# A hybrid decoder block: the state's update put ahead of the decay matrices' products, and the MLA heads' operands cast and split in two pieces

## The chip, the cores and the metric

One core of a Trainium2 chip. The metric is the device time of one execution in microseconds (us); the median of several executions is compared. TensorE (PE), VectorE (DVE), ScalarE (ACT) and GpSimd (POOL) each work through a queue of their own, in order; SP and ACT issue the DMAs.

## What is computed

One layer of a decoder trunk on 1,040 tokens (16 learned ones and 1,024 real ones), width 1,024. Three mixers stand side by side: stick-breaking attention (8 heads), a Mamba-2 state space mixer (SSD, 16 heads of 64, state 128, two groups), and MLA attention (8 heads, 64 + 32 columns per query and key). The two parts that the change touches:

```
# SSD, in chunks of 128 tokens; per group g of 8 heads
y_diag = einsum('bclsgj,bcsgjp->bclgjp', CB[..., None] * Ldec, X)
states = einsum('bclgn,bclgjp->bcgjpn', Bc, X * decay[..., None])
carry  = carry * chunk_decay + states              # chunk after chunk
y_off  = einsum('bclgn,bcgjpn->bclgjp', Cc, prev) * exp(Acs)
y      = y_diag + y_off

# MLA
s = einsum('bqhd,bkhd->bhqk', q, k) * scale        # q, k: 96 columns
o = softmax(mask(s)) @ v
```

After the mixers come the output projection and a gated feed-forward layer, each with a residual sum, and a last norm.

## The kernel before

Each dense product is made of three matmuls on fp32r operands, split in a high and a low half: `dense_fm` (L139 to L152; the matmuls are L147 to L149). Two PSUM banks (`d_ps`, pool `dpool`) take turns there; the engine that evacuates one sets when it is free.

A scheduler of the framework sets the order in which each engine gets its instructions. It goes through a simulated time line, and takes what is ready by the order in the program and by the priorities in it; so dense matmuls of later steps stand among the matmuls of the SSD chunks and of the MLA heads wherever these were not ready in its time line. They are called the fill here. What fills the SSD chunks is the latents' projection, the values `vtok` (L915 to L917) and the heads' key and query projections; what fills the MLA heads is the gate's projection (`gate_units`) and then the output projection (`out_rows`).

**SSD** (`ssd_chunk`, L765 to L856). Nine chunks, c = 0 to 8 (c = 0 has 16 tokens, and no `yo`, `yd` and `y`), each with two groups g. A group's chain:

- PE: eight small matmuls into two banks `R` (L802), which spread the running sums of the decays.
- ACT: `ea` (L811, four instructions: exp of the sums), `L` (L814, eight; then one exp over all of it, L824), and in between `dec` (L819).
- DVE: `L` times the masked product of the chunk's B and C (`cbm`, L829).
- PE: `yo` (L834, four matmuls): the chunk's C times the state `S[g]` as it stood before the chunk. DVE multiplies `ea` by it (L835).
- PE: `yd` (L838, eight matmuls): the decay matrices' products, X times `L`.
- POOL: `y += ea` (L843), then DVE: `y += yd` (L844).
- PE: `sps` (L847): the chunk's share of the state, from `Xd` (POOL, L820). POOL multiplies `S[g]` by the chunk's decay (L851), DVE adds `sps` (L854).

`yo`, `yd` and `sps` take turns in the two banks of the pool `yps`. There is one buffer for `ea` (tag `yt`, `bufs=1`): ACT writes a group's `ea` only when POOL has read the one of the group before. On POOL there stand, beside these, `y = xs * dsk` of a later chunk (L773), the low halves of weights (L136) and sums of squares (`grow`, L521).

**MLA** (`mla_load`, L963 to L980). Per head, the query (96 x 1024) and the key (96 x 1040) come by DMA into `st`, ACT casts each into `mhi` (L977), and POOL subtracts into `mlo` (L978). `mla_row` makes the scores from them (L997 to L999) and the exponentials `pr` on ACT (L1012); `weighted_values` transposes these (L319 to L331) and multiplies them by the values.

Of the kernel before, what the change touches and what calls it, by code (L numbers as in the profile page):

```python
# [11 lines left out]
F32 = mybir.dt.float32  # L12
# [3 lines left out]
ALU = mybir.AluOpType  # L16
# [43 lines left out]
def tile_hybrid_block(ctx: ExitStack, tc: tile.TileContext, a: dict):  # L60
    nc = tc.nc
    act, dve, pool, pe, sp = nc.scalar, nc.vector, nc.gpsimd, nc.tensor, nc.sync
# [6 lines left out]
    def f32(ap):  # L69
        return ap.bitcast(F32)  # L70
# [679 lines left out]
    with ExitStack() as st:  # L750
# [4 lines left out]
        yps = st.enter_context(tc.tile_pool(name="yps", bufs=2, space=PSUM, reuse_waits="tile"))  # L755
# [8 lines left out]
        def ssd_chunk(c):  # L764
            n = META if c == 0 else 128  # L765
            t0 = 0 if c == 0 else META + 128 * (c - 1)
            xs = p2.tile([128, 8, 128], F32, tag="xs", name="xs")
            bc = p2.tile([128, 4, 128], F32, tag="bc", name="bc")
            sp.dma_start(bc[:, :, :n], s_xs[8:12, :, t0 : t0 + n].rearrange("j p t -> p j t"))
            sp.dma_start(xs[:, :, :n], s_xs[0:8, :, t0 : t0 + n].rearrange("j p t -> p j t"))  # L770
            if c > 0:
                y = p2.tile([128, 8, 128], F32, tag="y", name="y")
                pool.tensor_tensor(y, xs, dsk.unsqueeze(2).to_broadcast([128, 8, 128]), op=ALU.mult)  # L773
            X = p2.tile([128, D], F32, tag="X", name="X")
            Xd = p2.tile([128, D], F32, tag="Xd", bufs=1, name="Xd")
            for g in range(2):
                gs = slice(512 * g, 512 * (g + 1))
                hs = slice(8 * g, 8 * g + 8)
                pt = tp.tile([128, 512], F32, tag="tp", name="xtp")
                for e in range(4):  # L780
                    pe.transpose(pt[:n, e * 128 : (e + 1) * 128], xs[:, 4 * g + e, :n], ident)
                dve.tensor_tensor(
                    heads(X[:n, gs]), heads(pt[:n]), DT[:n, c, hs].unsqueeze(2).to_broadcast([n, 8, 64]), op=ALU.mult
                )
            if c < 8:
                btok = p2.tile([128, 256], F32, tag="btok", bufs=1, name="btok")
                pt = tp.tile([128, 512], F32, tag="tp", name="btp")
                for g in range(2):
                    pe.transpose(pt[:n, g * 128 : (g + 1) * 128], bc[:, g, :n], ident)
                act.copy(btok[:n], pt[:n, :256])  # L790
            for g in range(2):
                gs = slice(512 * g, 512 * (g + 1))
                hs = slice(8 * g, 8 * g + 8)
                cd = p2.tile([128, 8], F32, tag="cd", name="cd")
                dec = p2.tile([128, 8], F32, tag="dec", name="dec")
                L = p2.tile([128, 8, 128], F32, tag="L", name="L")
                ea = p2.tile([128, 4, 128], F32, tag="yt", bufs=1, name="ea")
                for q in range(2):
                    R = rps.tile([128, 4, 128], F32, tag="R", name="R")
                    qs = slice(4 * q, 4 * q + 4)  # L800
                    for h in range(4):
                        pe.matmul(R[:, h, :n], sel[:, 8 * g + 4 * q + h, :], A3[:, t0 : t0 + n], start=True, stop=True)  # L802
                    if c < 8:
                        act.activation(cd[:, qs], R[:, :, n - 1], AF.Exp)
                        dve.tensor_tensor(
                            dec[:n, qs], R[:n, :, n - 1], AT[:n, c, 8 * g + 4 * q : 8 * g + 4 * q + 4], op=ALU.subtract
                        )
                    if c > 0:
                        for e in range(2):
                            half = slice(64 * e, 64 * e + 64)  # L810
                            act.activation(ea[half, 2 * q : 2 * q + 2], R[half, e::2, :], AF.Exp)  # L811
                        for h in range(4):
                            hh = 4 * q + h
                            act.activation(  # L814
                                L[:, hh, :], R[:, h, :], AF.Relu, scale=-1.0,
                                bias=AT[:, c, 8 * g + hh : 8 * g + hh + 1],
                            )
                if c < 8:
                    act.activation(dec[:n], dec[:n], AF.Exp)  # L819
                    pool.tensor_tensor(  # L820
                        heads(Xd[:n, gs]), heads(X[:n, gs]), dec[:n].unsqueeze(2).to_broadcast([n, 8, 64]), op=ALU.mult
                    )
                if c > 0:
                    act.activation(L, L, AF.Exp, scale=-1.0)  # L824
                    pcb = tp.tile([128, 512], F32, tag="tp", name="cbp")
                    pe.matmul(pcb[:, :128], bc[:, g, :], bc[:, 2 + g, :], start=True, stop=True)
                    cbm = p2.tile([128, 128], F32, tag="cbm", name="cbm")
                    dve.tensor_tensor(cbm, pcb[:, :128], tri, op=ALU.mult)
                    dve.tensor_tensor(L, L, cbm.unsqueeze(1).to_broadcast([128, 8, 128]), op=ALU.mult)  # L829
                    yo = yps.tile([128, 512], F32, tag="y", name="yo")  # L830
                    yd = yps.tile([128, 512], F32, tag="y", name="yd")
                    for j in range(4):
                        ts = slice(128 * j, 128 * (j + 1))
                        pe.matmul(yo[:, ts], S[g][:, ts], bc[:, 2 + g, :], start=True, stop=True)  # L834
                    dve.tensor_tensor(ea, ea, yo.rearrange("p (j t) -> p j t", j=4), op=ALU.mult)  # L835
                    for h in range(8):
                        hh = 8 * g + h
                        pe.matmul(  # L838
                            yd[64 * (h % 2) : 64 * (h % 2) + 64, 128 * (h // 2) : 128 * (h // 2 + 1)],
                            X[:, hh * 64 : (hh + 1) * 64], L[:, h, :], start=True, stop=True,  # L840
                        )
                    yg = y[:, 4 * g : 4 * g + 4]
                    pool.tensor_tensor(yg, yg, ea, op=ALU.add)  # L843
                    dve.tensor_tensor(yg, yg, yd.rearrange("p (j t) -> p j t", j=4), op=ALU.add)  # L844
                if c < 8:
                    sps = yps.tile([128, 512], F32, tag="y", name="sps")
                    pe.matmul(sps, btok[:n, g * 128 : (g + 1) * 128], Xd[:n, gs], start=True, stop=True)  # L847
                    if c == 0:
                        dve.tensor_copy(S[g], sps)
                    else:  # L850
                        pool.tensor_tensor(  # L851
                            heads(S[g]), heads(S[g]), cd.unsqueeze(2).to_broadcast([128, 8, 64]), op=ALU.mult
                        )
                        dve.tensor_tensor(S[g], S[g], sps, op=ALU.add)  # L854
            if c > 0:
                act.dma_start(s_y[:, :, 128 * (c - 1) : 128 * c].rearrange("j p t -> p j t"), y)  # L856

# [52 lines left out]
        for b, (t0, w) in enumerate(BLOCKS):  # L910
# [7 lines left out]
            t = row_tile("vtok")  # L918
# [18 lines left out]
        for c0, n in CH_SHORT:  # L937
            c = slice(c0, c0 + n)
# [3 lines left out]
            for half, (op, ta, tb) in enumerate(((ALU.subtract, ct, sn), (ALU.add, sn, ct))):  # L942
                t = fill_tile("cacc", "rope")
# [15 lines left out]
    with ExitStack() as st:  # L959
# [5 lines left out]
        def mla_load(h):  # L965
            p, hr = h // 2, slice(64 * (h % 2), 64 * (h % 2) + 64)
            out = []
            for cols, parts in (
                (SEQ, [(s_qn[p, hr], 0, 64), (s_qr[0, 16 * h : 16 * h + 16], 64, 80), (s_qr[1, 16 * h : 16 * h + 16], 80, 96)]),
                (T, [(s_kn[p, hr], 0, 64), (s_krot, 64, 96)]),  # L970
            ):
                raw = ml.tile([128, T], F32, tag="st", name="st")
                for src, r0, r1 in parts:
                    sp.dma_start(raw[r0:r1, :cols], src)
                hi = ml.tile([128, T], F32R, tag=f"hi{cols}", name="mhi")
                lo = ml.tile([128, T], F32R, tag=f"lo{cols}", name="mlo")
                act.copy(hi[:96, :cols], raw[:96, :cols])  # L977
                pool.tensor_tensor(lo[:96, :cols], raw[:96, :cols], f32(hi[:96, :cols]), op=ALU.subtract)  # L978
                out += [hi, lo]
            return out  # L980

# [143 lines left out]
    cols = ctx.enter_context(tc.tile_pool(name="cols", bufs=1, side="right", reuse_waits="tile"))  # L1125
# [69 lines left out]
    for kt in range(4):  # L1195
        hi, lo = homes[kt]
# [581 lines left out]
```

## Time and profile before

| | |
|---|---|
| three executions | 1761.19, 1754.87, 1760.85 us; median 1760.85 |
| the profiled execution | 1762.44 us, of which its span is 1760.7 us |
| busy in the span | PE 1706.4 us (97%), DVE 1140.2, ACT 846.2, POOL 720.0 |
| granted TensorE clock, mean | 0.986 of 2.4 GHz |
| SSD chunks, from the first `yo` to the last | 490.4 to 637.4 us |
| MLA heads, scores | 665.7 to 1001.1 us |

In the time line of the profile a row is an instruction or several that were merged: its start and duration in us, the engine, the line, the operation, and in brackets how long the engine was idle just before and what ended that. A matmul's duration overlaps with the next one's; how far PE gets is read from the starts.

### The profile page before, as it was taken

The page shows a single profiled execution, that of the slowest core. Times are in us where ns is not written, and L with a number is a line of the kernel's source. Part 1 is how long each engine was busy: PE and PEld are TensorE (multiplying, and loading weights), DVE is VectorE, ACT ScalarE, POOL GpSimd, SP SyncE. Part 2 cuts the span into 40 slices and gives each one's busy share as a digit, 9 for nine tenths or more (in the row PEclk, how much of TensorE's full clock was granted, in tenths as well). Part 3 has the DMA queues.
Part 4 walks back from the last instruction along what each step waited for, and adds up shares of the span by engine and source line. Part 5 has one row for each costly group of instructions (what it writes and reads, how often), then busy time and mean ns, then how long its engine had stood idle before and what let it go on. Part 6 is the DMA issues. An engine that isn't in the chain of part 4 may idle for free. (4 is left out here: it accounts for less than half of the span.)

```text
span 1760.7 us, 26573 instructions
## 1 busy us (share of the span) xinstructions
PE 1706.4 (97%) x9801; PEld 1500.3 (85%) x9801; DVE 1140.2 (65%) x1742; ACT 846.2 (48%) x1797; POOL 720.0 (41%) x498
## 2 busy tenths in 40 slices
PE   8979999999999899999999999999999999999998
PEld 7969989999987788998888888778888888878887
DVE  7778666678444663555575655986566666688644
ACT  7546565655467646675454425432222232244332
POOL 3334346344466657563321346544455545200012
PEclk9989999999999999999999998999999999999998
DMA  4312232122533645347330443123333223999702
GB/s 162 82 56 64 71 86 79 58 71 73 156 111 115 200 157 154 108 125 244 110 91 29 124 155 102 60 84 101 109 102 102 96 90 104 314 370 386 254 1 97
DMA packets 145639, 222.35 MB, mean 126 GB/s; under 512 B 24722, under 2 KB 84148, under 8 KB 145508
## 3 DMA queue, kind: packets, MB, share of 16 engines
q1 hardware_dynamic: 126112, 205.09, 35.9%
q10 hardware_dynamic: 19396, 15.56, 2.9%
q8 instruction: 77, 1.26, 0.3%
q14 instruction: 54, 0.44, 0.1%
HBM read 157.56 MB, written 63.04 MB: 125 GB/s over the span
## 5 line engine op out<-in xcount | busy, mean ns | idle before, releaser
L147 PE MATMUL d_ps<-hnh,whi 128*128 128x384 f32 (+6 forms) x744 | 250.1, 336 | 7.4 <-DVE KS L610 4.7
L149 PE MATMUL d_ps<-hnl,whi 128*128 128x384 f32 (+6 forms) x744 | 246.7, 332 | 0.0
L148 PE MATMUL d_ps<-hnh,wlo 128*128 128x384 f32 (+6 forms) x744 | 245.8, 330 | 0.0
L136 POOL TENSOR_TENSOR wlo<-wraw,whi 128x1024 fp32r<-128x1024 f32 (+1 forms) x57 | 138.0, 2420 | 222.7 <-ACT whi L134 218.3
L147 PEld LDWEIGHTS d_ps<-hnh,whi 128*128 128x128 f32 (+1 forms) x744 | 141.0, 190 | 12.5 <-issue 6.1
L148 PEld LDWEIGHTS d_ps<-hnh,wlo 128*128 128x128 f32 (+1 forms) x744 | 141.2, 190 | 2.8 <-issue 0.5
L149 PEld LDWEIGHTS d_ps<-hnl,whi 128*128 128x128 f32 (+1 forms) x744 | 140.9, 189 | 2.8 <-issue 0.2
L1285 PE MATMUL b_ps<-T,wl 128*128 128x512 f32 x352 | 138.8, 394 | 1.3 <-POOL wl L1116 1.3
L1286 PE MATMUL b_ps<-T,wh 128*128 128x512 f32 x352 | 138.2, 394 | 1.3 <-DVE T L1116 1.3
L1284 PE MATMUL b_ps<-T,wh 128*128 128x512 f32 x352 | 139.1, 396 | 0.0
L315 DVE TENSOR_TENSOR pl<-ptg,ph 128x512 fp32r<-128x512 f32 (+1 forms) x160 | 99.3, 627 | 48.2 <-ACT ph L314 46.9
L1115 ACT CAST op<-raw 128x1024 fp32r<-128x1024 f32 x69 | 71.3, 1050 | 107.4 <-PE d_ps L1570 59.2
L1116 DVE TENSOR_TENSOR op<-raw,op 128x1024 fp32r<-128x1024 f32 x69 | 84.8, 1239 | 39.0 <-ACT op L1115 38.9
L704 DVE TENSOR_TENSOR_SCAN cm<-cm,zcol 128x144 f32<-128x144 f32 (+3 forms) x64 | 101.7, 1593 | 12.3 <-ACT cm L702 11.9
L314 ACT CAST ph<-ptg 128x512 fp32r<-128x512 f32 (+1 forms) x160 | 85.2, 543 | 39.9 <-PE ptg L331 24.7
L1116 POOL TENSOR_TENSOR wlo<-raw,whi 128x1024 fp32r<-128x1024 f32 x18 | 45.6, 2531 | 110.0 <-ACT whi L1115 110.0
L1116 POOL TENSOR_TENSOR wl<-raw,wh 128x512 fp32r<-128x512 f32 x46 | 74.4, 1625 | 29.2 <-ACT wh L1115 29.2
L1115 ACT CAST wh<-raw 128x512 fp32r<-128x512 f32 x88 | 53.1, 615 | 67.2 <-PE b_ps L1286 67.1
L1122 POOL TENSOR_TENSOR tt<-tt 128x512 f32<-128x512 f32 (+1 forms) x8 | 8.1, 1011 | 186.1 <-ACT tt L1640 185.9
L1012 ACT ACTIVATE pr<-sc_ps,sm 128x256 f32<-128x256 f32 (+4 forms) x112 | 59.8, 540 | 46.8 <-DVE sm L1009 24.8
L1285 PEld LDWEIGHTS b_ps<-T,wl 128*128 128x128 f32 x352 | 66.5, 189 | 16.8 <-POOL wl L1116 1.6
L502 DVE SCALAR_TENSOR_TENSOR cacc<-d_ps,cw,cacc 128x384 f32<-128x384 f32 (+3 forms) x108 | 61.7, 571 | 29.5 <-ACT cacc L495 27.4
(442 smaller groups left out, 5180.8 us busy)
## 6 DMA issues: line engine op xcount, KB each, us to landing
raw<-in_w_down_dram SPq DMA_DIRECT2D x99, 256.0 KB, 5.3
s_hops<-gs SPq DMA_DIRECT2D x63, 256.0 KB, 2.0
raw<-s_hops SPq DMA_DIRECT2D x63, 256.0 KB, 5.4
raw<-in_w_gate_dram SPq DMA_DIRECT2D x22, 512.0 KB, 3.6
raw<-in_w_up_dram SPq DMA_DIRECT2D x22, 512.0 KB, 4.1
wraw<-in_w_o_dram SPq DMA_DIRECT2D x16, 512.0 KB, 4.5
wraw<-in_w_xbc_dram SPq DMA_DIRECT2D x12, 512.0 KB, 3.6
s_xs<-csig SPq DMA_DIRECT2D x24, 192.0 KB, 1.9
```

Of the source, the lines that this page charges most:

```text
L136: pool.tensor_tensor(lo[:, :cols], raw[:, :cols], f32(hi[:, :cols]), op=ALU.subtract)
L147: pe.matmul(ps[:m, :n], wh, mh, start=(kt == 0), stop=False)
L148: pe.matmul(ps[:m, :n], wl, mh, start=False, stop=False)
L149: pe.matmul(ps[:m, :n], wh, ml, start=False, stop=(kt == nkt - 1))
L314: act.copy(ph[:, :n], pt[:, :n])
L315: dve.tensor_tensor(pl[:, :n], pt[:, :n], f32(ph[:, :n]), op=ALU.subtract)
L704: dve.tensor_tensor_scan(rev, rev, zcol.to_broadcast([128, n_all]), 1.0, ALU.mult, ALU.add)
L1115: act.copy(hi, value)
L1116: eng.tensor_tensor(lo, value, f32(hi), op=ALU.subtract)
L1284: pe.matmul(banks[j], hi[:, ks], UH[u][k], start=start and k == 0, stop=False, skip_group_check=skip)
L1285: pe.matmul(banks[j], lo[:, ks], UH[u][k], start=False, stop=False, skip_group_check=skip)
L1286: pe.matmul(banks[j], hi[:, ks], UL[u][k], start=False, stop=stop and k == 3, skip_group_check=skip)
```

## The change

In `ssd_chunk` the block from `sps` to the sum into `S[g]` stands ahead of the block with `yd` and the two sums into `y`. In `mla_load` each operand is cast and split in two pieces of columns, 0 to 511 and the rest (512 or 528).

```diff
                     yo = yps.tile([128, 512], F32, tag="y", name="yo")
-                    yd = yps.tile([128, 512], F32, tag="y", name="yd")
                     for j in range(4):
                         ts = slice(128 * j, 128 * (j + 1))
                         pe.matmul(yo[:, ts], S[g][:, ts], bc[:, 2 + g, :], start=True, stop=True)
                     dve.tensor_tensor(ea, ea, yo.rearrange("p (j t) -> p j t", j=4), op=ALU.mult)
-                    for h in range(8):
-                        hh = 8 * g + h
-                        pe.matmul(
-                            yd[64 * (h % 2) : 64 * (h % 2) + 64, 128 * (h // 2) : 128 * (h // 2 + 1)],
-                            X[:, hh * 64 : (hh + 1) * 64], L[:, h, :], start=True, stop=True,
-                        )
-                    yg = y[:, 4 * g : 4 * g + 4]
-                    pool.tensor_tensor(yg, yg, ea, op=ALU.add)
-                    dve.tensor_tensor(yg, yg, yd.rearrange("p (j t) -> p j t", j=4), op=ALU.add)
                 if c < 8:
                     sps = yps.tile([128, 512], F32, tag="y", name="sps")
                     pe.matmul(sps, btok[:n, g * 128 : (g + 1) * 128], Xd[:n, gs], start=True, stop=True)
...
                         dve.tensor_tensor(S[g], S[g], sps, op=ALU.add)
+                if c > 0:
+                    yd = yps.tile([128, 512], F32, tag="y", name="yd")
+                    for h in range(8):
+                        hh = 8 * g + h
+                        pe.matmul(
+                            yd[64 * (h % 2) : 64 * (h % 2) + 64, 128 * (h // 2) : 128 * (h // 2 + 1)],
+                            X[:, hh * 64 : (hh + 1) * 64], L[:, h, :], start=True, stop=True,
+                        )
+                    yg = y[:, 4 * g : 4 * g + 4]
+                    pool.tensor_tensor(yg, yg, ea, op=ALU.add)
+                    dve.tensor_tensor(yg, yg, yd.rearrange("p (j t) -> p j t", j=4), op=ALU.add)
...
-                act.copy(hi[:96, :cols], raw[:96, :cols])
-                pool.tensor_tensor(lo[:96, :cols], raw[:96, :cols], f32(hi[:96, :cols]), op=ALU.subtract)
+                for c in (slice(0, 512), slice(512, cols)):
+                    act.copy(hi[:96, c], raw[:96, c])
+                    pool.tensor_tensor(lo[:96, c], raw[:96, c], f32(hi[:96, c]), op=ALU.subtract)
                 out += [hi, lo]
```

The scheduler then moves more than the block. In the new program's lines `sps` is L837, `S` L841, `yd` L849, `y += ea` L854, `y += yd` L855, the casts L979 and L980, the scores L999 to L1001.

The first place is PE in the SSD chunks, at chunk 6's first group. Before (`yd` of the group, and `sps` right behind it):

```order
L149 MATMUL d_ps_7408<-llo_7234,whi_7351 128x272
L838 MATMUL yd_6358<-L_6321,X_6300 64x128 x8
L847 MATMUL sps_6374<-Xd_6301,btok_6314 128x512
L147 MATMUL d_ps_7416<-lhi_7227,whi_7351 128x384
L148 MATMUL d_ps_7416<-lhi_7227,wlo_7353 128x384
L149 MATMUL d_ps_7416<-llo_7228,whi_7351 128x384
```

The same place in the changed program:

```order
L149 MATMUL d_ps_7356<-llo_7234,whi_7351 128x272
L789 MATMUL btp_6459<-identr_88,bc_6439 128x128 x2
L849 MATMUL yd_6367<-L_6321,X_6300 64x128 x8
L833 MATMUL yo_6416<-bc_6295,S1_5504 128x128 x4
L826 MATMUL cbp_6496<-bc_6439 128x128
L147 MATMUL d_ps_7364<-lhi_7227,whi_7351 128x384
```

The next group's `yo` stands right behind `yd` now, and `sps` of this group stands some 20 rows ahead of this `yd`. The fill is an earlier one: from the first `yo` to the last there are 144 fill matmuls of 384 columns, 66 of 256 and 24 of 272 in either program, but 54 of 512 columns where there were 117; the other 63 stand behind the chunks.

The second place is POOL at chunk 4 (`y_6010`; `ea_6034` and `ea_6093` are its two groups, and `y_6154` is chunk 5's). Before:

```order
L820 TENSOR_TENSOR Xd_6013<-X_6012,dec_6032 128x512
L170 TENSOR_TENSOR rc_7209<-rc_7209,mhalf_96 128x8
L851 TENSOR_TENSOR S0_5503<-S0_5503,cd_6031 128x512
L773 TENSOR_TENSOR y_6154<-xs_6150,dsk_5501 128x1024
L843 TENSOR_TENSOR y_6010<-y_6010,ea_6034 128x512
L820 TENSOR_TENSOR Xd_6013<-X_6012,dec_6091 128x512
L851 TENSOR_TENSOR S1_5504<-S1_5504,cd_6090 128x512
L843 TENSOR_TENSOR y_6010<-y_6010,ea_6093 128x512
```

Now:

```order
L841 TENSOR_TENSOR S0_5503<-S0_5503,cd_6031 128x512
L820 TENSOR_TENSOR Xd_6013<-X_6012,dec_6032 128x512
L854 TENSOR_TENSOR y_6010<-y_6010,ea_6034 128x512
L136 TENSOR_TENSOR wlo_7353<-wraw_7349,whi_7351 128x1024
L521 TENSOR_TENSOR grow_5484<-grow_5484,sq_7197 128x256
L773 TENSOR_TENSOR y_6154<-xs_6150,dsk_5501 128x1024
L841 TENSOR_TENSOR S1_5504<-S1_5504,cd_6090 128x512
L854 TENSOR_TENSOR y_6010<-y_6010,ea_6093 128x512
```

The scaling of `xs` moves behind the first group's `y += ea`, and stands, with a weight's low half and a sum of squares, ahead of the second group's. It moves behind `y += ea` of the first group in the same way at chunk 6 (`y_6442`, chunk 7's, behind `ea_6322`), and stays ahead of it at chunk 3 (`y_6010`, with a sum of squares, ahead of `ea_5890`) and at chunk 7 (`y_6586` ahead of `ea_6466`).

The third place is ACT where the sixth MLA head's operands are cast, at the end of the gate's fill. Before:

```order
L314 CAST ph_8878<-ptg_8874 128x384
L977 CAST mhi_9338<-st_9335 96x1040
L977 CAST mhi_9331<-st_9327 96x1024
L339 COPY half_8886<-pv_8841 64x256
L1012 ACTIVATE pr_8908,sm_8909<-sc_ps_8910,sm_8909 128x272
```

Now:

```order
L1014 ACTIVATE pr_8907,sm_8908<-sc_ps_8914,sm_8908 128x512
L979 CAST mhi_9360<-st_9357 96x512
L979 CAST mhi_9360<-st_9357 96x528
L979 CAST mhi_9351<-st_9347 96x512 x2
L339 COPY half_8902<-pv_8857 64x256
L1014 ACTIVATE pr_8924,sm_8925<-sc_ps_8926,sm_8925 128x272
```

The four pieces stand in a row, with nothing of another kind between them; so they do at all eight heads on ACT, but for one pair of the second head, and in POOL's queue the pieces of one operand stand together as well.

## Rows read from the trace of the kernel before

**Rows 1.** The page's first part: busy time, share of the span and number of instructions of PE and its weight loads.

```profile
PE 1706.4 (97%) x9801; PEld 1500.3 (85%) x9801; DVE 1140.2 (65%) x1742; ACT 846.2 (48%) x1797; POOL 720.0 (41%) x498
```

**Rows 2.** Busy time of each engine in stretches: start and end, length, PE, its weight loads, DVE, ACT, POOL (with instructions), granted clock, DMA share, GB/s. Two stretches of 10 us, then the SSD chunks from the first `yo` to the last.

```profile
540.00:550.00 10.00, 7.47 (x50) 6.46 (x51) 4.23 (x6) 7.86 (x24) 7.35 (x6) 0.68 0.26 81
820.00:830.00 10.00, 9.42 (x53) 9.26 (x54) 4.55 (x8) 5.84 (x17) 4.81 (x3) 0.66 1.03 331
...
490.40:637.40 147.00, 137.37 (x1010) 114.32 (x1009) 84.76 (x138) 96.49 (x277) 92.75 (x64) 0.98 0.45 143
```

**Rows 3.** What PE waited for between 470 and 660 us: us in total, times, longest.

```profile
PE yd L838 <- DVE L L829: 4.7, 8, 1.2
PE R L802 <- ACT L L814: 2.3, 4, 1.4
PE yo L834 <- DVE y L844: 1.4, 1, 1.4
PE d_ps L176 <- ACT lrow L743: 0.6, 1, 0.6
PE d_ps L149 <- DVE llo L881: 0.4, 1, 0.4
```

**Rows 4.** What ACT and POOL waited for between 500 and 645 us, the longest of each.

```profile
ACT ea L811 <- POOL y L843: 22.3, 9, 4.0
...
POOL y L843 <- DVE ea L835: 10.2, 4, 5.7
```

**Rows 5.** The time line at chunk 3: POOL, then ACT and PE.

```profile
534.45 2.37 POOL L773 TENSOR_TENSOR y<-xs,dsk 128x1024 f32<-128x1024 f32 x1 [3.37 <-issue]
536.78 1.04 POOL L851 TENSOR_TENSOR S<-S,cd 128x512 f32<-128x512 f32 x1
537.78 1.00 POOL L521 TENSOR_TENSOR grow<-grow,sq 128x384 f32<-128x384 f32 x1
538.75 1.27 POOL L843 TENSOR_TENSOR y<-y,ea 128x512 f32<-128x512 f32 x1
...
540.06 0.77 ACT L811 ACTIVATE ea<-R 64x256 f32<-64x256 f32 x2 [4.01 <-POOL y L843]
...
543.84 0.58 PE L802 MATMUL R<-A,sel 80*128 80x128 bf16 x4 [1.42 <-ACT L L814]
```

**Rows 6.** The time line at chunk 6: POOL, ACT, and the three waits of PE.

```profile
594.13 1.90 POOL L773 TENSOR_TENSOR y<-xs,dsk 128x1024 f32<-128x1024 f32 x1 [6.12 <-DVE nope L894]
595.99 1.04 POOL L851 TENSOR_TENSOR S<-S,cd 128x512 f32<-128x512 f32 x1
596.99 1.27 POOL L843 TENSOR_TENSOR y<-y,ea 128x512 f32<-128x512 f32 x1
...
598.30 0.77 ACT L811 ACTIVATE ea<-R 64x256 f32<-64x256 f32 x2 [3.72 <-POOL y L843]
...
599.04 1.16 PE L834 MATMUL yo<-bc,S 128*128 128x128 f32 x8 [1.37 <-DVE y L844]
602.08 0.38 PE L802 MATMUL R<-A,sel 80*128 80x128 bf16 x4 [0.39 <-ACT L L814]
604.43 1.09 PE L838 MATMUL yd<-L,X 128*64 128x128 f32 x16 [0.86 <-DVE L L829]
```

**Rows 7.** PE's time line: `yo` of chunk 5's two groups, and two fill matmuls of 512 columns.

```profile
571.46 1.11 PE L834 MATMUL yo<-bc,S 128*128 128x128 f32 x8
579.39 0.78 PE L834 MATMUL yo<-bc,S 128*128 128x128 f32 x5
...
555.19 0.39 PE L917 MATMUL d_ps<-wlo,lhi 128*16 128x512 f32 x1
555.42 0.39 PE L915 MATMUL d_ps<-whi,lhi 128*16 128x512 f32 x1
```

**Rows 8.** Groups of instructions by line and form: busy us, mean ns of one, idle before. The MLA operands' casts and splits, and pieces of 512 columns of the same kind elsewhere.

```profile
L977 ACT CAST mhi<-st 96x1024 fp32r<-96x1024 f32 x8 | 8.4, 1044 | 4.2 <-DMA st<-s_qr 3.8 <-DMA st<-s_kn 0.4
L1115 ACT CAST wh<-raw 128x512 fp32r<-128x512 f32 x88 | 53.1, 615 | 67.2 <-PE b_ps L1286 67.1
L978 POOL TENSOR_TENSOR mlo<-st,mhi 96x1024 fp32r<-96x1024 f32 x8 | 19.1, 2392 | 0.8 <-ACT mhi L977 0.8
L231 POOL TENSOR_TENSOR wk<-raw,wk 128x512 fp32r<-128x512 f32 x1 | 1.3, 1277 | 4.0 <-ACT wk L230 4.0
L1116 POOL TENSOR_TENSOR wl<-raw,wh 128x512 fp32r<-128x512 f32 x46 | 74.4, 1625 | 29.2 <-ACT wh L1115 29.2
```

**Rows 9.** The time line at the first MLA head (POOL, DVE) and at the sixth head's casts (ACT, PE).

```profile
664.17 4.82 POOL L978 TENSOR_TENSOR mlo<-st,mhi 96x1024 fp32r<-96x1024 f32 x2
668.93 1.04 POOL L548 TENSOR_TENSOR gy<-gy,gs 128x384 f32<-128x384 f32 x1
...
670.00 0.56 DVE L550 TENSOR_TENSOR go<-d_ps,gy 128x384 f32<-128x384 f32 x1 [5.20 <-POOL gy L548]
...
817.52 2.00 ACT L977 CAST mhi<-st 96x1040 fp32r<-96x1040 f32 x2 [0.64 <-PE sc_ps L998]
...
820.58 0.38 PE L319 MATMUL ptm<-identr,pr 128*16 128x128 f32 x1 [2.00 <-ACT pr L1012]
```

**Rows 10.** What PE waited for between 660 and 1040 us, the longest.

```profile
PE ptm L319 <- ACT pr L1012: 2.2, 2, 2.0
```

## The prediction

> **What bounds the kernel now.** The page's first part comes first: PE is busy 1706.4 us, 97% of the span, and the next engine, DVE, 65% [rows 1]. So the time changes only where PE waits or where its clock falls. The matmuls are the same before and after; an earlier operand anywhere else is worth nothing unless a wait of PE ends with it. The change touches two stages, and each is read by itself.
>
> The SSD chunks last 147.0 us from the first `yo` to the last [rows 2]: 16 groups, 15 periods of 9.8 us. ACT is busy there 96.5 us, POOL 92.75, DVE 84.8, some 6 us of each group, so none of the three is full. PE's waits of that stage are five kinds, 4.7 + 2.3 + 1.4 + 0.6 + 0.4 = 9.4 us [rows 3]; and in one stretch of 10 us the granted clock is 0.68, between the two levels of 1.2 and 2.4 GHz, which costs at most 10 x 0.32 = 3.2 us [rows 2]. What stands behind most of these waits is seen on ACT: it waits 22.3 us in 9 times to write `ea`, because POOL has not yet read the one before; and POOL waits 10.2 us for DVE's product [rows 4]. There is one buffer for `ea`. Where POOL has something else ahead of `y += ea`, this loop stretches. At chunk 3 that is the scaling of `xs` (2.37 us), `S` and a sum of squares: ACT waits 4.01 us, and PE 1.42 us soon after [rows 5]. At chunk 6 the scaling begins at 594.13 and `y += ea` only at 596.99; ACT waits 3.72 us, and PE 1.37 + 0.39 + 0.86 = 2.6 us at three places until 604.43 [rows 6].
>
> In the MLA heads the reader is to look for a wait of PE on the split operands. There is none among the longest; the longest is of the transposes for `pr`, 2.2 us in two times [rows 10].
>
> **Part 1, the state's block ahead of the decay matrices' products.** The block is one matmul (`sps`), one POOL multiplication (`S`) and one DVE sum per group, with no DMA; `yd`, `y += ea` and `y += yd` slip behind it, and behind the last of these the store of `y`, whose reader comes long after the chunks. No instruction is added, so the direct cost is nothing; what counts is order.
>
> *On POOL.* At chunk 6 the scaling of `xs` moves behind the first group's `y += ea`. That sum can then start some 1.9 us earlier, at about the end of `S`, which itself needed only PE's `yo` [rows 6]. The 1.37 us of `yo` go twice over: it waited for the bank which `y += yd` freed, and now the banks turn as `yo`, `sps`, `yd`, so that the next `yo` takes over the bank of `sps`. ACT's `ea` and `L` follow earlier, and the 0.39 and 0.86 us behind them go too: **-2.6 us**. At chunk 3 the scaling and the sum of squares still stand ahead of `y += ea`, and I leave the waits of 1.42 us and the low clock as they are [rows 5]. At chunk 4 the scaling goes behind the first `y += ea` but comes to stand, with a weight's low half, ahead of the second: a gain and a loss of the same size, taken as 0.
>
> *On PE.* Between the first `yo` and the last there are 63 fill matmuls of 512 columns fewer. One of these takes 0.23 us by the starts of two neighbours, 555.19 and 555.42 [rows 7]. So 63 x 0.23 = 14.5 us of fill move behind the chunks. They cost PE the same there; the stage would be shorter by 14.5 us if nothing else set its pace. PE's own work in the stage is 147.0 - 9.4 = 137.6 us now, and 137.6 - 14.5 = 123.1 us then, 8.2 us per group. Can the other engines keep that? The quickest group in the trace took 579.39 - 571.46 = 7.9 us [rows 7], and the three engines' busy shares of 6 us allow it. The ends: if every wait goes, -9.4 us (with the clock, -12.6); if the groups keep their 9.8 us although the fill is gone, +14.5 us. The point at which nothing is won or lost is a mean period of (123.1 + 9.4) / 15 = 8.8 us. I take the groups to follow at about that pace, since the fastest period lies below it and the mean of 9.8 contains 0.97 us of fill that leaves it and 0.6 us of waits: 9.8 - 0.97 is the same 8.8. So nothing for this and the 2.6 us from chunk 6 remain.
>
> A rule bears on this stage. The Trainium skill, Perfetto Trace Analysis, section Optimization Strategy, takes consistent bubbles as a sign of too few buffers; the change adds none, so by that rule the stage would keep its waits (rival B). The row with one buffer's wait, 22.3 us on ACT, speaks for it.
>
> **Part 2, the casts and splits in two pieces.** Eight heads with two operands each get 16 casts and 16 subtractions more. On ACT a piece of 512 columns takes 615 ns where it is of the same kind elsewhere, the whole 1044 ns: 2 x 615 - 1044 = 186 ns more per operand, 0.37 us per head. On POOL a subtraction of 512 columns took 1277 or 1625 ns, the whole 2392 ns: 0.16 to 0.86 us more per operand, 0.3 to 1.7 us per head [rows 8]. What can it gain? A score could start on the first piece; but no wait of PE for a split operand is among the trace's [rows 10], so 0. What can it cost? It costs where ACT's or POOL's burst delays somebody. One such place is at 817.52: two casts of 2.00 us in a row, and PE waits 2.00 us for `pr` at 820.58 [rows 9]; the clock of that stretch is 0.66 [rows 2]. With four pieces in a row, as they stand on ACT, the burst is 0.37 us longer, and so is the wait. The other is at the first head: POOL's two subtractions take 4.82 us, then comes `gy` at 668.93, and DVE's `go`, which frees the fill's bank, waits 5.20 us for that [rows 9]. There I take the lower price, 2 x 0.16 = 0.32 us, since 1277 ns is nearest to half of 2392. Elsewhere ACT (48%) and POOL (41%) have room [rows 1]. Together **+0.7 us**; bounds are -2.0 (the wait at 820.58 goes) and 0.37 + 1.7 = +2.1.
>
> A rule speaks for the split. The Trainium skill, Perfetto Trace Analysis, section Optimizing Scalar/DVE Operations, advises to break up instructions where Scalar or Vector are not saturated but cause bubbles on other engines. By it the wait behind the burst would halve, -1.0 in place of +0.37; that would need something to pass between the pieces, and the order has them back to back.
>
> **Sum.** The profiled execution took 1762.4 us. 1762.4 - 2.6 + 0.7 = 1760.5. It stands 1.6 us above the median of the runs shown, 1760.85; so against that median I forecast 1760.5 - 1.6 = **1758.9 us**, 0.1% less. A measurement of this kernel can tell about 0.5% from no change, 8.8 us.
>
> **The rivals.**
> *A, the forecast*: the chunk 6 waits go, the rest keeps pace. Its own range is 1753 to 1765 (1758.9 and 6 to either side, half of the stage's ends). Chance 0.42.
> *B, nothing happens*: the one buffer for `ea` goes on setting the waits, in other places than before, as POOL's order moves a stall from one group to the next; the stage keeps its 9.4 us. 1762.4 + 0.7 - 1.6 = 1761.5. For it: the buffer is untouched, and the scaling merely changes its place at chunk 4. Against it: chunk 6. Chance 0.15.
> *C, all waits go*: with the banks' turn changed and `S` earlier, no group waits any more, and the clock does not fall either: 1762.4 - 9.4 - 3.2 + 0.7 - 1.6 = 1748.9. For it: the largest kind, `yd` behind `L` (4.7 us), gets more room, as `sps` now stands some 20 rows ahead of `yd`. Against it: chunk 3's order stays. Chance 0.26.
> *D, slower*: the order puts the groups closer together, with less fill between them, than the loop over `ea` (ACT, DVE, POOL, ACT) lets them go. PE then waits out the time in which fill stood before. If the groups keep 9.8 us, all 14.5 us turn into waits: 1762.4 + 14.5 + 0.7 - 1.6 = 1776.0. It decides from a period of 8.8 us on, and is worth 0.5% from (123.1 + 9.4 + 8.1) / 15 = 9.4 us. For it: ACT's 22.3 us of waiting show that the loop, not ACT's work, sets its pace already. Against it: the period of 7.9 us. Chance 0.17.
>
> **How the numbers follow.** A and B lie within 0.5%: 0.57. C is faster by over 0.5%: 0.26. D is slower by that: 0.17. The range goes from a little below C (1748.9, less 3.9 for a clock that holds elsewhere too, since 820 to 830 shows 0.66 as well) to the middle of the way from A to D and somewhat beyond, at a period of 9.5 us: 1745 to 1772. Left out is the upper half of D and what no case holds.
>
> **What would show it.** Right: in the chunks the first `yo` to the last take about 130 us; ACT's waits for `ea` fall from 22 us, and at chunk 6 PE has no wait of over 0.5 us at `yo`; at chunk 3 the 1.42 us and the low clock are there still; PE has the 63 fill matmuls behind the chunks at 0.23 us each; the cast's pieces take some 0.6 us, and PE's longest wait for `pr` is 2.0 to 2.4 us. Wrong: a stage of 140 us or more with waits for `L`, `ea` or a bank of over 15 us (D); a stage below 124 us (C); PE waiting for a piece `mlo` or `mhi`, which part 2 says never occurs; or a difference in the gate, the output projection or the feed-forward layer, where I count nothing.

## The result

The changed kernel took 1749.45 us (median of 8 executions, 1742.89 to 1751.59), the kernel before 1760.07 us (8 executions). The ratio is 0.9937, with a 95% interval of 0.9925 to 0.9949: 0.6% faster, outside the 0.5% that the forecast of 1758.9 us stood for. The time lies in the range, on the side of rival C. It did not get there in rival C's way alone.

### The profile page after: what moved, and what is told of

It reads as the page before. It is cut to its first block, busy times and chain, and to the rows that moved or that the text cites. A ratio compares the mean times of both kernels' runs of the same rounds, so it can differ in the third digit from the quotient of the medians.

```text
span 1745.5 us, 26611 instructions
## 1 busy us (share of the span) xinstructions
PE 1697.1 (97%) x9801; PEld 1491.2 (85%) x9801; DVE 1136.4 (65%) x1742; ACT 847.0 (49%) x1813; POOL 717.3 (41%) x514
## 5 line engine op out<-in xcount | busy, mean ns | idle before, releaser
L134 ACT CAST whi<-wraw 128x1024 fp32r<-128x1024 f32 (+1 forms) x57 | 58.9, 1034 | 58.7 <-PE d_ps L149 33.5
L1121 DVE TENSOR_TENSOR raw<-raw 128x512 f32<-128x512 f32 x58 | 54.3, 947 | 42.2 <-DMA raw<-in_w_gate_dram 39.5
L1288 PEld LDWEIGHTS b_ps<-T,wh 128*128 128x128 f32 x352 | 66.3, 188 | 16.6 <-DVE T L1118 1.6
```

The source lines that it names most:

```text
L1288: pe.matmul(banks[j], hi[:, ks], UL[u][k], start=False, stop=stop and k == 3, skip_group_check=skip)
```

## The profile after

The profiled execution took 1747.19 us. Its page's first part, against [rows 1]:

```profile
PE 1697.1 (97%) x9801; PEld 1491.2 (85%) x9801; DVE 1136.4 (65%) x1742; ACT 847.0 (49%) x1813; POOL 717.3 (41%) x514
```

The 9801 matmuls are the same, yet PE is busy 9.3 us less. The span fell by 15.2 us, so PE's idle time fell only by 5.9. The same matmuls in less time points to the clock: the mean granted clock is 0.986 before and 0.993 after. Part of the 15.2 is the two executions: the first `yo` comes 3.1 us earlier although everything up to there is the same.

The table by stages needs two cuts that mean the same in both programs: the first `yo`, the first score, and the first matmul of the feed-forward layer's second product. Between these PE has the same 3739 matmul records in both. Columns as in [rows 2]; before:

```profile
490.38:665.66 175.28, 164.29 (x1173) 139.65 (x1173) 97.75 (x163) 109.60 (x304) 105.29 (x76) 0.98 0.47 148
665.66:1108.90 443.24, 434.57 (x2567) 388.88 (x2567) 252.78 (x493) 236.30 (x544) 188.68 (x121) 0.98 0.40 121
```

After, with the chunks alone (first `yo` to the last) in the third row:

```profile
487.27:659.07 171.80, 163.26 (x1170) 138.61 (x1169) 94.31 (x163) 107.89 (x303) 105.25 (x76) 0.98 0.47 150
659.07:1094.70 435.63, 428.93 (x2570) 383.55 (x2571) 252.45 (x494) 238.47 (x560) 187.88 (x137) 0.99 0.40 124
...
487.27:610.45 123.18, 119.40 (x947) 100.16 (x947) 71.16 (x130) 94.20 (x277) 84.41 (x61) 1.00 0.45 139
```

So 3.5 us went in the first stretch and 7.6 us in the second, which the prediction had down for +0.7. PE's idle time is the length less its busy time. It fell from 10.99 to 8.54 us in the first stretch and from 8.67 to 6.70 in the second; the other 1.0 and 5.6 us are PE being busy for less time with all but the same matmuls, an estimate of what the clock gave.

**The chunks.** They last 123.2 us instead of 147.0, a period of 8.2 us, which is the pace that the prediction worked out for PE without any wait. That the two agree is partly luck: PE still idles 123.18 - 119.40 = 3.8 us of it, and the low clock that the prediction's 137.6 us contained (3.2 us) is not there. What PE waited for, from the first `yo` to the feed-forward layer (us, times, longest), against [rows 3] (the kinds of the heads are left out):

```profile
PE d_ps L147 <- ACT lrow L743: 2.7, 1, 2.7
...
PE d_ps L176 <- DVE nope L895: 1.4, 1, 1.4
PE d_ps L147 <- DVE rope L946: 1.2, 1, 1.2
...
PE yd L849 <- DVE L L829: 0.9, 2, 0.6
PE sc_ps L999 <- ACT mhi L979: 0.8, 1, 0.8
...
PE R L802 <- ACT L L814: 0.4, 1, 0.4
```

`yd` behind `L` fell from 4.7 us in 8 times to 0.9 in 2. One group (chunk 5's second) shows how. Before: DVE finishes `L` at 584.62, and PE, which had been standing there for 1.13 us, starts `yd` at 584.67.

```profile
582.61 2.01 DVE L829 TENSOR_TENSOR L<-L,cbm 128x1024 f32<-128x1024 f32 x1 [1.31 <-ACT L L824]
...
584.67 1.09 PE L838 MATMUL yd<-L,X 128*64 128x128 f32 x16 [1.13 <-DVE L L829]
```

The same group after: `L` is done at 569.39, and PE comes to `yd` 1.67 us later, without a wait, since matmuls of other work now stand ahead of it.

```profile
567.74 1.65 DVE L829 TENSOR_TENSOR L<-L,cbm 128x1024 f32<-128x1024 f32 x1 [2.71 <-ACT L L824]
...
571.06 1.09 PE L849 MATMUL yd<-L,X 128*64 128x128 f32 x16
```

At chunk 3 the loop over `ea` is as it was in [rows 5]: the scaling and the sum of squares stand ahead of `y += ea`, and ACT waits 3.65 us. But no wait of PE of over 0.4 us is left behind it:

```profile
526.71 1.90 POOL L773 TENSOR_TENSOR y<-xs,dsk 128x1024 f32<-128x1024 f32 x1 [0.57 <-DMA s_y<-y]
528.57 1.00 POOL L521 TENSOR_TENSOR grow<-grow,sq 128x384 f32<-128x384 f32 x1
529.52 1.27 POOL L854 TENSOR_TENSOR y<-y,ea 128x512 f32<-128x512 f32 x1
...
530.83 0.77 ACT L811 ACTIVATE ea<-R 64x256 f32<-64x256 f32 x2 [3.65 <-POOL y L854]
```

From the last `yo` to the first score it then takes 48.6 us instead of 28.3: 14.5 us of it are the 63 fill matmuls, and the rest is mostly one new wait, 2.67 us for a row of norms (`lrow`), with a low clock behind it (PE's row, then stretches with the granted clock as in [rows 2]):

```profile
614.28 0.79 PE L147 MATMUL d_ps<-lhi,whi 128*128 128x512 f32 x1 [2.67 <-ACT lrow L743]
```

```profile
614.00:615.00 1.00, 0.72 (x2) 0.63 (x3) 1.00 (x1) 1.00 (x3) 0.79 (x2) 0.50 0.74 290
615.00:620.00 5.00, 5.00 (x14) 3.84 (x13) 3.94 (x2) 0.66 (x1) 5.00 (x2) 0.50 0.26 104
```

So of 23.8 us won in the chunks 14.5 are fill that stands elsewhere, and some 6 are given back there (2.67 of the wait, and by an estimate 3 of a clock at half of 2.4 GHz).

At the very end of that stretch stands one of the prediction's own signs of being wrong: the first score waits for a piece `mhi`, which part 2 says never occurs.

```profile
659.07 0.68 PE L999 MATMUL sc_ps<-mhi 96*128 96x144 f32 x3 [0.85 <-ACT mhi L979]
```

**The heads.** The sixth head, where [rows 9] had a burst of two casts and PE's wait of 2.00 us for `pr`:

```profile
809.89 2.19 ACT L979 CAST mhi<-st 96x512 fp32r<-96x512 f32 x4 [0.91 <-PE sc_ps L1000]
...
811.46 2.05 PE L176 MATMUL d_ps<-identr,rc 128*128 128x128 f32 x16 [1.06 <-POOL rc L170]
813.34 0.27 PE L319 MATMUL ptm<-identr,pr 128*16 128x128 f32 x1
```

ACT's burst is longer (2.19 us for four pieces), as the prediction said. But PE does not wait for `pr` there: 16 matmuls of the gate's norms, which before stood behind this place (from 822.57 on), fill it, after a wait of 1.06 us of their own. The clock of 0.66 in the stretch behind it is gone (1.00 from 812 to 822).

## The experiments

Ratios are against the kernel before, timed beside them, with 95% intervals.

**The two parts alone.** The first kernel keeps the whole operands, the second the old chunks.

```diff
 # e1: as the changed kernel, but in mla_load
-                for c in (slice(0, 512), slice(512, cols)):
-                    act.copy(hi[:96, c], raw[:96, c])
-                    ...
+                act.copy(hi[:96, :cols], raw[:96, :cols])
+                pool.tensor_tensor(lo[:96, :cols], raw[:96, :cols], f32(hi[:96, :cols]), op=ALU.subtract)
```

> Only the state's block is moved; the MLA operands stay whole. Theory 1 (the two parts act separately, each in its own stage): from the first yo to the first score the trace of the changed kernel was 3.5 us shorter, so about 1756.5 us against 1760.1 before; the wait of 2.0 us for pr at the sixth head and the low clock behind it are still there. Rival (the moved block alone brings everything, because the 63 fill matmuls that moved behind the chunks fill the MLA heads' gaps): about 1749.5 us, and no wait of 2 us at the sixth head.

Measured: 1756.81 us, 0.9981 (0.9969 to 0.9992).

> Only the casts and splits are in two pieces; the chunks' order is that of before. Theory 1: from the first score to the feed-forward layer the changed kernel was 7.6 us shorter, so about 1752.5 us, the chunks keep about 175 us from the first yo to the first score, and there is no wait of over 0.5 us for pr at the sixth head. Rival (the moved block brings everything): 1760.1 to 1761 us, as the prediction's second part had it (+0.7 us).

Measured: 1752.47 us, 0.9956 (0.9938 to 0.9973). The product of the two ratios is 0.9937, the ratio of both together: the parts add up, and theory 1 holds in size. The orders show why they can: e1's order on PE is that of the changed kernel through the chunks but for four rows, e2's is that of the changed kernel from the first score to the end. But e1's order in the heads is neither before's nor the changed kernel's, so the moved block does not act on the chunks alone. The same stretches, e1 first, then e2:

```profile
490.70:661.06 170.36, 161.43 (x1173) 137.26 (x1173) 94.45 (x163) 108.17 (x303) 105.69 (x76) 1.00 0.48 152
661.06:1103.80 442.74, 431.00 (x2566) 385.38 (x2566) 255.71 (x493) 236.00 (x545) 188.67 (x121) 0.98 0.40 122
```

```profile
488.02:662.23 174.21, 163.37 (x1170) 138.33 (x1169) 98.56 (x163) 108.73 (x304) 104.72 (x76) 0.98 0.46 148
662.23:1101.80 439.57, 432.03 (x2570) 386.02 (x2571) 253.10 (x494) 238.26 (x560) 188.04 (x137) 0.98 0.40 123
```

The rows show less than the times do. Of the 7.2 us between e2's profile and before's only 3.7 lie in the heads' stretch, and only 1.1 of these are idle time (8.67 and 7.54); 2.4 us lie ahead of the first `yo`, where PE's order is the same.

e1 wins 4.9 us in the first stretch, where its clock is 1.00 all along although PE waits 2.6 us for `lrow` there as well, and in the second PE's idle time is 442.74 - 431.00 = 11.7 us, 3.1 more than before. Most of that is one place, at the end of the output projection, where nothing else is left for PE:

```profile
1030.38 0.80 PE L1386 MATMUL d_ps<-raw,whi 128*128 128x512 f32 x1 [3.04 <-DVE hT L1095]
```

Before has no such wait, nor have e2 and the changed kernel, where 12 matmuls of `out_rows` are left to stand between the last product's first matmuls and this one.

**A second buffer for `ea`**, in the changed kernel (`bufs=1` to `bufs=2` on tag `yt`).

> The changed kernel with two buffers for ea instead of one. Theory 1 (what is left of waits in the chunks comes from other places: lrow, the rotary and norm rows): the waits of ACT for ea (11.7 us) go, PE gets back at most the 0.9 + 0.5 + 0.4 us for L and ea; 1747.5 to 1749.5 us. Rival (the one buffer sets the stage's pace, the row of ACT's waits for ea): all 6.5 us of waits in the chunks and the 3.3 us of low clock at 613 to 620 go, about 1740 us.

Measured: 1748.19 us, 0.9935 (0.9917 to 0.9953), the changed kernel's ratio. ACT's 11.7 us of waits for POOL's `y += ea` go, and 13.7 us of waits for DVE's `dec` stand in their place. The order changed with the buffer: the chunks last only 112.65 us, more fill stands behind them, and PE waits 4.0 us for `lhi` there. Up to the first score it is 170.55 us with 8.99 us of idle time, where the changed kernel has 171.80 and 8.54. So the buffer's waits were not what kept PE idle in the changed kernel, and the rival falls. That they were not in the kernel before is argued from this and from chunk 3: no run gave that kernel a second buffer. Its trace has other links as long beside those of [rows 4], where POOL's longest wait is not shown:

```profile
ACT dec L819 <- DVE dec L805: 13.8, 8, 3.3
...
POOL Xd L820 <- ACT dec L819: 10.8, 3, 5.5
```

**What of the split counts?** Six kernels vary the pieces in the changed kernel, with the chunks as they are.

```diff
 # e4: casts in pieces, one subtraction
+                for c in (slice(0, 512), slice(512, cols)):
+                    act.copy(hi[:96, c], raw[:96, c])
+                pool.tensor_tensor(lo[:96, :cols], raw[:96, :cols], f32(hi[:96, :cols]), op=ALU.subtract)
 # e5: one cast, subtractions in pieces
 # e6, e8: in pieces for h != 5, for h == 0
 # e7: pieces of 256 columns
 # e9: whole for h in (3, 5, 6, 7)
```

> The changed kernel with the casts in two pieces, but one whole subtraction on POOL per operand. Theory 1a (the order that follows from ACT's pieces is the gain, not the pieces' earlier ends): 1749 to 1750 us, as the changed kernel. Rival 1b (POOL's pieces let the scores start earlier): the gain of the MLA heads goes, about 1756.5 us, and PE waits for mlo or pr over 1 us somewhere in the heads.

Measured: 1751.07 us, 0.9951 (0.9934 to 0.9969). By the time the subtraction's pieces can be left out: the interval overlaps the changed kernel's and ends below rival 1b's 1756.5 us, though 1a's own range is missed by 1 us. Its cause does not follow: the order in the heads is another one than the changed kernel's, and PE waits 1.8 us for `mhi` and 3.4 us for `pr` in the heads (0.8 and 1.7 in the changed kernel).

> The changed kernel with whole casts on ACT and only POOL's subtractions in two pieces. But for 34 rows at the first heads PE's order is that of the kernel with the moved block alone (1756.8 us). Theory S1 (the gain of the heads comes from the order that the scheduler makes when ACT's casts are in pieces: it fills places where PE waited, and the low clock behind them goes): about 1757 us, with the wait of 2.0 us for pr at the sixth head. Rival S2 (the pieces' earlier ends are the gain): some of the 7.7 us, 1750 to 1754 us.

Measured: 1753.6 us, 0.9968 (0.9956 to 0.9981). The time lies in S2's range of 1750 to 1754 us; the interval overlaps e1's as well: undecided by the time. In its profile the heads' stretch is 443.1 us (e1 442.7), with the 2.0 us for `pr` and a wait of 3.4 us at the output projection's end; its span gained on e1's ahead of the first `yo`, where the programs are alike.

> The changed kernel with the sixth head's operands whole again, the other seven in pieces. PE's order is that of the changed kernel but for four rows. S1 (order): as the changed kernel, 1749.5 us, no wait of over 1.2 us at the sixth head. S2 (pieces): the 2.0 us wait at that head is back, with 3.4 us of low clock, about 1752 to 1755 us.

Measured: 1750.15 us, 0.9952 (0.9937 to 0.9966). The sixth head's own pieces are not what ended its wait: whole operands, the changed order, and PE's wait for `pr` is 0.4 us. That wait speaks for S1; the time alone does not decide, since the interval reaches into S2's range.

> The changed kernel with four pieces of 256 (the last 272) columns per operand in place of two. S2 (earlier ends are worth it): at least the gain of two pieces, 1749 us or less. S1: the order is a new one, so the result is not tied to the number of pieces; between 1750 and 1758 us, with ACT and POOL each some 2 to 4 us busier in all and PE's waits at other heads.

Measured: 1755.62 us, 0.9979 (0.9967 to 0.9992): more pieces, and most of the gain lost. The heads' stretch is 442.4 us again, with 4.1 us at the output projection's end. S2's 1749 us or less falls here.

> The changed kernel with pieces at the first head alone. S2 (each head's pieces bring their share): an eighth of 7.7 us, about 1755.8 us. S1: the pieces of one head already turn the whole order of the heads, so the gain is not an eighth: anywhere from 1749 to 1758 us, and the time goes with the waits of PE and the low-clock stretches between the first score and the feed-forward layer.

Measured: 1755.23 us, 0.9984 (0.9971 to 0.9996), as S2 has it too. S1 allowed nearly any time here; what speaks for it is that the order is another one, with 3.7 us at the output projection's end.

> The changed kernel with four of the eight heads' operands whole (the fourth, sixth, seventh and eighth head), the others in pieces. PE's order is that of the changed kernel but for 48 rows. S1 (the order is the gain): 1749 to 1751 us, the first score to the feed-forward layer 434 to 437 us. S2 (pieces that end earlier are the gain): half of the 7.7 us lost, about 1753.3 us.

Measured: 1749.57 us, 0.9945 (0.9927 to 0.9963). Half of the heads lost their pieces, and the time stayed, 4 us from S2's figure, which the interval's upper end just reaches. The stretch was 440.7 us in the profile, a miss against 434 to 437; PE's idle time in it is the changed kernel's (440.67 - 433.92 = 6.75 us, there 6.70), and the rest is a lower clock in that execution, the slowest of its six.

Put side by side, PE's idle time in the heads sorts by order and not by pieces. The rows of e6 and e9:

```profile
660.36:1096.45 436.09, 429.24 (x2570) 383.40 (x2571) 251.35 (x493) 237.42 (x558) 188.61 (x135) 0.99 0.40 124
660.73:1101.40 440.67, 433.92 (x2570) 387.32 (x2571) 253.43 (x493) 237.29 (x552) 187.72 (x129) 0.98 0.40 123
```

| PE's order in the heads | kernels | stretch, us | PE idle in it, us |
|---|---|---|---|
| the changed kernel's | changed, e2, e3, e11 | 435.6, 439.6, 434.5, 439.0 | 6.7, 7.5, 7.3, 7.8 |
| the same but for 4 and 48 rows | e6, e9 | 436.1, 440.7 | 6.9, 6.8 |
| others (e5's is e1's but for 34 rows) | before, e1, e4, e5 | 443.2, 442.7, 438.3, 443.2 | 8.7, 11.7, 9.4, 13.6 |
| others | e7, e8, e12 | 442.4, 443.6, 440.5 | 10.6, 10.8, 8.7 |

So PE's idle time goes with the order. Against before that is 1 to 2 us; the rest of what these kernels won there is PE busy for less time, which is the clock. And e4, with more idle time there than before, still has the ratio 0.9951: its granted clock is 0.9922 in the mean of its executions, against 0.9875 before.

**Where `yd` stands.** One kernel puts `yd`'s eight matmuls ahead of `yo`, the other puts `yd` and its sum off until the next group's state update.

```diff
 # e10: yd ahead of yo
+                    yd = yps.tile(...)
+                    for h in range(8): pe.matmul(yd[...], X[...], L[:, h, :], ...)
                     yo = yps.tile([128, 512], F32, tag="y", name="yo")
 # e11: yd of the group before, behind this group's S
+                if pend:
+                    pend.pop()()
                 if c > 0:
...
+                    pend.append(late)   # late: yd, y += yd, the store of y
```

> The changed kernel with the decay matrices' products (yd) put ahead of yo, and so further ahead of sps than in the kernel before. Theory Y (the chunks' gain comes from yd standing later on PE, when its L is done): PE waits for L 5 us or more in the chunks, in 8 groups or more, and the first yo to the first score takes 174 us or more. Rival (the state S being ready earlier, or POOL's and DVE's order, brought it): the waits for L stay near the 0.9 us of the changed kernel, and the stretch near 171 us. The heads' order changes as well, so the total says little: 1749 to 1762 us.

Measured: 1803.97 us, 1.0255 (1.024 to 1.0271). PE's longest waits from the first `yo` to the first score:

```profile
PE yd L833 <- DVE L L829: 19.2, 8, 8.4
PE R L802 <- ACT L L814: 16.6, 9, 3.8
```

The stretch is 216.6 us, against 175.3 before. Theory Y holds, far beyond its figure: the total missed the expected 1749 to 1762 us by 42. The waits for `R`, nearly as long, were not part of it, and the fill stands otherwise as well.

> The changed kernel with each group's yd and its sum into y put off until the next group's state update. The heads' order is that of the changed kernel. Theory Y: the 0.9 us of waits for L and the 0.5 us for ea go, nothing else is left there, so 1748 to 1749.5 us. If the later sums into y hold up the banks or the stores of y instead, PE waits for a bank behind DVE's sum: 1751 to 1755 us.

Measured: 1746.59 us, 0.9927 (0.9913 to 0.9941), the lowest of all; its interval overlaps the changed kernel's, so it beats before, and is not shown to beat the change. The stretch:

```profile
486.12:654.68 168.56, 162.36 (x1170) 138.12 (x1169) 94.19 (x163) 110.15 (x304) 106.41 (x77) 0.98 0.49 154
```

PE does not wait for `L` at `yd` at all there, and its idle time is 6.2 us (8.5 in the changed kernel). Its wait for `lrow` is 0.3 us, too, so the 3.2 us that this stretch is shorter are not `yd`'s alone.

**The new wait for the row of norms.**

```diff
-            act.activation(row[:, c0 : c0 + m], ps[:, :m], AF.Copy, scale=scale)
+            dve.tensor_scalar(row[:, c0 : c0 + m], ps[:, :m], scale, None, op0=ALU.mult)
```

> The changed kernel with the rows of norms (lrow) evacuated by DVE instead of ACT, against the longest wait in the chunks, 2.7 us for ACT's lrow with the low clock at 613 to 620 behind it. If that wait is ACT's queue: it goes, 2.7 to 6 us less, 1744 to 1747 us, unless the order of the heads, which also changes, gives it back. If DVE's queue is as late (its 2.8 us for llo stand there too): no gain in the chunks, 1749 to 1755 us.

Measured: 1747.8 us, 0.9937 (0.992 to 0.9954). The 2.7 us for `lrow` are gone and the stretch is 168.6 us; waits for `L` came to 2.7 us, the heads' stretch is 440.4 us. Won in one place and given back in the other, as the expectation allowed.

Two more edits change nothing: with `sps` alone ahead of `yd` in the text (the update of `S` left behind), or with `y += ea` written ahead of `sps`, every engine gets exactly the changed kernel's order. Of the moved block only the place of `sps` against `yd` counts.

## Why the prediction was right in its range and wrong in its steps

- *What bounds it*: right. The time moved with PE's waits and its clock. But the forecast's sum counted nothing for the clock (rival C had 3.2 us of it, the range's lower end 3.9 more), and it carries most of the gain: over all executions its mean is 0.9875 before (54) and 0.9922 after (8); 0.0047 of 1760 us is an estimate of 8 us, of a difference of 10.6. In the two profiles it is 9.3 of 15.2. The same estimate gives e1 some 6 us (mean 0.9908, 12 executions) and e2 some 5 (0.9905, 6); that is more than e1's whole gain, and the two do not add up to 8. So the clock is not tied to either part.
- *Part 1, size*: -2.6 us was forecast. The first stretch gave -3.5 us in the changed kernel and -4.9 us in e1, and e1 as a whole -0.19% (3.3 us). That this is near is luck: it is what is left of some 9 us won in the chunks and some 6 given back behind them, and the sum has neither. The chunks were to take about 130 us and took 123.2; at chunk 3 the wait of 1.42 us and the low clock were to stay and are gone. That the groups follow the thinner fill held: 8.2 us, so rival D is out.
- *Part 1, cause*: wrong. The step that failed is the reading of ACT's 22.3 us for `ea` [rows 4] as what stood behind PE's waits. In the changed kernel a second buffer won nothing, and chunk 3's stall of ACT (3.65 us) is still there without PE's. The largest kind, `yd` behind `L` [rows 3], was named under rival C; of its 4.7 us the forecast priced only chunk 6's 0.86. It is the one that went most, from 4.7 to 0.9 us, since `yd` now comes later on PE: put earlier it waits 19.2 us (e10), put later still not at all (e11).
- *Rival C* was right about the chunks' length (123.2 us, below its bound of 124), though 3.8 us of idle time are left in them, and wrong about the end: some 6 us came back at `lrow` behind them. That the total came out within 1 us of its 1748.9 is luck: it had +0.7 for part 2.
- *Part 2*: this is the term that was mis-sized, +0.7 us forecast against -0.44% (7.7 us) for the split alone. The price of a piece held (619 ns on ACT where 615 was taken); back to back, four took 2.19 us where 4 x 615 ns would be 2.46. What failed is the sentence that an earlier operand gains nothing because no wait for an operand is in the trace: it took the order of the heads as given. With the pieces the scheduler makes another order, from the first score to the feed-forward layer. That the order, and not the pieces' earlier ends, goes with PE's idle time there is what e6 and e9 (fewer pieces, nearly the same order, the same idle time) and e7 (more pieces, another order, gain lost) show. That it brings the whole 7.7 us is not shown: the idle time is 1 to 2 us of it, the rest goes with the clock.
- *The Trainium skill's rules*. The Trainium skill, Perfetto Trace Analysis, section Optimizing Scalar/DVE Operations, says that breaking up instructions may let work be completed sooner where Scalar or Vector are not saturated but cause bubbles on other engines; the prediction put that at -1.0 us at the sixth head. The wait did go, yet with the sixth head whole as well (e6), and four pieces did worse than two (e7), so these runs are no evidence for it. The Trainium skill, Perfetto Trace Analysis, section Optimization Strategy, says of a gap that repeats on the engine that should be saturated that it can mean too few buffers. The prediction took ACT's 22.3 us for such a case, but the engine that is full here is PE; a second `ea` gave 0.9935, one gave 0.9937, so for this buffer the reading does not hold in the changed kernel.
- *Open*: which waits bring the low clock. Before, 2.00 us of waiting ended at 820.58, and the clock is 0.50 right behind it; e1 has the same wait at 815.68, with PE's order the same for some 160 matmuls ahead of it and 33 behind, and a clock of 1.00:

```profile
821.00:822.00 1.00, 1.00 (x7) 1.00 (x5) 0.16 (x1) 0.88 (x4) 1.00 (x1) 0.50 1.02 385
```

```profile
816.00:818.00 2.00, 2.00 (x20) 2.00 (x19) 1.16 (x4) 1.95 (x9) 2.00 (x2) 1.00 1.02 390
```

So how much of the clock's 8 us is due to which removed wait, or to any, is not settled. Nor was the heads' new order tried with all operands whole, nor a second `ea` in the kernel before.

## What to carry to other kernels

Where a scheduler orders the instructions, an edit's price is that of the new order, not of the instructions that it adds: compare the orders over the whole program, and look at each place where PE runs out of other work. Here, on an engine that is full, the product whose operand is late did best standing late: from the first `yo` to the first score it took 216.6 us with `yd` ahead of `yo`, 175.3 behind `yo`, 171.8 behind `sps` too. A long wait of an engine that is not the bound (ACT's 22 us) says nothing until a wait of the bound is seen to end with it. And before a cause is given for a difference of 0.5%, part it into idle time and clock: here most of it was the clock, whose cause no run settled.

## What was not expected of the hardware

In e10 the granted clock of TensorE was 0.50, the lower of its two levels, for all of the 20 us from 700 to 720, with PE busy 9.4 us of them, and 0.89 from the first `yo` to the first score: beside the 36 us of waits stands, by an estimate, 0.11 x 216.6 = 24 us of lost clock. Which wait brought which part of it is not shown.

```profile
498.08:714.69 216.61, 175.19 (x1163) 148.97 (x1162) 90.79 (x156) 110.69 (x297) 105.84 (x79) 0.89 0.40 129
700.00:720.00 20.00, 9.37 (x51) 8.27 (x48) 4.63 (x7) 6.04 (x17) 4.45 (x7) 0.50 0.06 17
```
